# A hybrid decoder layer on one core: transposes of the second half in the products' PSUM banks, one head's loads on another queue, and two channel pairs of the up projection interleaved

## The chip, the cores and the metric

One NeuronCore of one Trainium2 chip. The metric is the device time of one execution in microseconds (us). Engines are named as in the profile: PE (TensorE, products and transposes), DVE (VectorE), ACT (ScalarE), POOL (GpSimd), SP (SyncE, which only issues DMAs here). PE's granted clock is given as a share of 2.4 GHz; its two levels are 1.00 (2.4 GHz) and 0.50 (1.2 GHz).

## The reference

One layer over 2048 tokens of width 1024, all in float32:

```python
h = rms(x, norm_mix_g);  z = h @ w_in + b_in            # columns for three groups of mixers
oa = forgetting_attention(rms(q), rms(k), v, cumsum(log_sigmoid(f)))   # 8 heads of 64
ob = mlstm_chunkwise(silu(conv4(b_qk)), b_v, b_i, b_f)                 # 4 heads of 64, chunks of 64
oc = hgrn2_chunkwise(silu(c_q), log_f, c_i)                            # 4 heads of 64, chunks of 16
y = concat(rms(oa), sigmoid(b_o) * rms(ob), silu(c_g) * rms(oc)) * out_g
x = x + y @ w_out
u = conv3(rms(x, norm_ffn_g) @ w_up) + conv_b;  gate, up = split(u)    # 2 x 2816 channels
out = x + (silu(gate) * up) @ w_down
```

## The kernel before

Every product of float32 operands is made of three products of split operands: `hi` (rounded, "fp32r") and `lo` (the rest), as hi·hi + lo·hi + hi·lo. ACT writes `hi`, and DVE or POOL subtracts to get `lo`.

**In-projection and mixers.** The tokens go in two halves of 1024, each of two blocks of 512. For a half, `z_norm` loads token tiles of 128 tokens (`z_load`, L225, a ring of two buffers tagged `x`), scales them (L163, DVE) and transposes them into `hhi`/`hlo` (`to_T`: eight transposes per tile in two groups of four, L174; ACT copies each group at L176, DVE subtracts at L177). The rstd of all eight tiles of the second half is made ahead by `z_stats`. `z_groups` then runs over 14 column groups of `w_in`; its products are at L215, 512 columns wide for the groups `c0 c1 b0 b1` and 256 narrow for the others. The product banks have the tag `w`, a ring of three in PSUM. The transposes of the norm and those of `qk_norm_T` (L427, which follow the q and k groups and wait for their own rstd chain) share the tag `t`, a ring of two; a `t` bank comes free when DVE has subtracted (L177 or L434).

`merge` runs the mixers' steps (mLSTM: L578 to L635; HGRN: L727 to L799) between the groups' steps: chains of small products on PE with work of DVE and ACT in between. The second half's first L727 needs the `c` columns of that half. Outside attention the order of instructions on each engine is the scheduler's, made when the kernel is built; attention's order is written out.

**Attention.** Eight heads in the order 4 5 6 7 0 1 2 3, over steps `t`. A step makes the scores of 128 keys by up to 512 queries (L936, L937; two PSUM banks tagged `s`), the exponential (L943) and a copy (L945) on ACT, the rest on POOL or DVE (L949), and, three steps later, the products with V (L962 to L964). `att_maxima` runs ahead (L886). `att_load` loads a head's QA, KA, QB, KB and V by ten DMAs from what the in-projection stored (`s_qh`, `s_kh`, `s_v`, ...), all on SP (L851); the next head's are issued at a written step, for the second head after the step (1, 2) of the first, the seventh. DMAs rotate over eight semaphores, so the ninth and tenth wait until the first and second have landed.

**Up projection.** The product by `w_up` is done by Strassen's scheme on 2 x 2 blocks: seven block products per pair of channel tiles (L1339), each 12 matmuls of 512 columns, named by the h-blocks `b11 b21 t1 t2 t3 t4 b22`. `up_blocks` loads four blocks of weights (L1302), makes four sums (L1313, DVE) and splits seven blocks (L1307 ACT, L1308 POOL). `h_unit` makes the h-blocks; `t3` and `b22` are split at its L1228 (DVE and POOL) while the first products run. `ffn_up` goes over pairs 0, 11, 1, 12, ...; a pair's two PSUM tiles (four in all) are emptied by the convolution (L1353 to L1355). For each pair of pairs POOL also makes sums of `w_down` (`w_blocks`, L1441).

## Time and profile before

| | us |
|---|---|
| median of 3 runs | 2878.68 (2875.48 to 2880.37) |
| profiled execution | 2879.12 |
| its span | 2877.0 (the other 2.1 lie around it) |
| PE busy | 2788.7, 97% |
| DVE, ACT, POOL busy | 1938.7 (67%), 1277.4 (44%), 1481.5 (51%) |
| mean granted clock of PE | 0.982 |

A row of the profile names a line of the code, an engine, what it writes and reads (out<-in) and times. "Idle before, releaser" is how long the engine stood before an instruction, and what ended that. A PE row's duration is longer than its share of time, since products overlap; the distance between starts is what one costs.

### The profile page before, as it was taken

What the parts mean: (1) busy time and instruction counts of PE and PEld (TensorE: products, weight loads), DVE (VectorE), ACT (ScalarE), POOL (GpSimd) and SP (SyncE); (2) the same over time, 40 slices, a digit from 0 to 9 for tenths busy, and PEclk for the clock granted to TensorE, in tenths of its full rate; (3) what the DMA queues carried; (4) which work ended last, traced back from release to release, by engine and by line L of the source; (5) the groups of instructions that cost most, each with busy time, mean ns of one, the idle gap of its engine ahead of it and who ended that gap; (6) DMA issues with size and microseconds to landing.
All of it is one profiled execution on the core that took longest, in us unless ns stands there. A gap on an engine that the chain in (4) does not pass through costs nothing. (4 is left out here: it accounts for less than half of the span.)

```text
span 2877.0 us, 42992 instructions
## 1 busy us (share of the span) xinstructions
PE 2788.7 (97%) x15053; PEld 2337.0 (81%) x15053; DVE 1938.7 (67%) x3523; ACT 1277.4 (44%) x2167; POOL 1481.5 (51%) x1451
## 2 busy tenths in 40 slices
PE   7999998999998999999999899999999999999999
PEld 7899996889997766776787688888788788888887
DVE  6336786264777787777446677776786677777655
ACT  4214322141322888888223444444454344434443
POOL 2346562344564678777001666665476445444443
PEclk9999997999998999999999999999999999999999
DMA  5424434333336534641456445545678333333766
GB/s 161 131 91 138 150 122 137 102 93 111 98 103 182 107 90 90 131 88 26 150 180 204 137 160 169 168 155 181 233 253 278 98 99 100 106 110 128 238 210 207
DMA packets 347160, 411.06 MB, mean 143 GB/s; under 512 B 47682, under 2 KB 234128, under 8 KB 344032
## 3 DMA queue, kind: packets, MB, share of 16 engines
q1 hardware_dynamic: 292560, 318.45, 37.3%
q10 hardware_dynamic: 51952, 81.45, 7.8%
q0 software_dynamic: 2432, 8.42, 0.8%
q8 instruction: 118, 1.93, 0.3%
q14 instruction: 98, 0.80, 0.1%
HBM read 280.24 MB, written 127.98 MB: 142 GB/s over the span
## 5 line engine op out<-in xcount | busy, mean ns | idle before, releaser
L1308 POOL TENSOR_TENSOR w<-w,w 128x512 fp32r<-128x512 f32 x302 | 403.2, 1349 | 404.6 <-ACT w L1307 349.4
L1496 PE MATMUL ps<-w,w 128*128 128x512 f32 x1848 | 423.3, 391 | 3.9 <-ACT w L1487 2.6
L1496 PEld LDWEIGHTS ps<-w,w 128*128 128x128 f32 x1848 | 348.2, 189 | 78.2 <-ACT w L1487 3.0
L215 PE MATMUL w<-whi,hhi 128*128 128x256 f32 (+1 forms) x1280 | 369.7, 289 | 2.7 <-DVE z L332 2.5
L215 PE MATMUL w<-wlo,hhi 128*128 128x256 f32 (+1 forms) x1280 | 370.2, 290 | 0.0
L215 PE MATMUL w<-whi,hlo 128*128 128x256 f32 (+1 forms) x1280 | 369.0, 288 | 0.0
L949 POOL TENSOR_TENSOR pl<-pf,ph 128x512 fp32r<-128x512 f32 (+2 forms) x240 | 288.4, 1218 | 110.1 <-ACT ph L945 73.7
L1489 POOL TENSOR_TENSOR w<-w,w 128x512 fp32r<-128x512 f32 x154 | 215.5, 1406 | 205.4 <-ACT w L1487 152.7
L1307 ACT ACTIVATE w<-w 128x512 fp32r<-128x512 f32 x302 | 180.7, 628 | 258.4 <-POOL w L1308 87.1
L1488 DVE TENSOR_TENSOR w<-w,w 128x512 fp32r<-128x512 f32 x154 | 177.0, 1159 | 110.1 <-ACT w L1486 103.9
L215 PEld LDWEIGHTS w<-whi,hhi 128*128 128x128 f32 x1280 | 245.0, 191 | 5.1 <-DVE z L332 3.0
L215 PEld LDWEIGHTS w<-whi,hlo 128*128 128x128 f32 x1280 | 244.8, 191 | 1.6 <-issue 0.2
L215 PEld LDWEIGHTS w<-wlo,hhi 128*128 128x128 f32 x1280 | 245.2, 192 | 0.7
L198 POOL TENSOR_TENSOR wlo<-wraw,whi 128x256 fp32r<-128x256 f32 (+1 forms) x224 | 171.7, 804 | 107.0 <-ACT whi L195 79.8
L1313 DVE TENSOR_TENSOR w<-w,w 128x512 f32<-128x512 f32 x176 | 149.6, 869 | 80.9 <-DMA w<-in_w_up_dram 74.3
L943 ACT ACTIVATE pf<-s 128x512 f32<-128x512 f32 (+1 forms) x320 | 172.2, 538 | 70.4 <-PE s L937 22.3
L945 ACT ACTIVATE ph<-pf 128x512 fp32r<-128x512 f32 (+1 forms) x320 | 185.1, 579 | 10.2
L901 DVE TENSOR_REDUCE mx<-m 128x1 f32<-128x512 f32 x192 | 130.6, 685 | 64.5 <-PE m L886 61.8
L1354 DVE SCALAR_TENSOR_TENSOR u<-ps,fcol,u 128x1023 f32<-128x1023 f32 x88 | 108.9, 1278 | 95.2 <-ACT u L1353 95.2
L1487 ACT ACTIVATE w<-w 128x512 fp32r<-128x512 f32 x154 | 96.6, 628 | 111.2 <-PE ps L1496 87.7
L1486 ACT ACTIVATE w<-w 128x512 fp32r<-128x512 f32 x154 | 95.9, 623 | 92.7 <-POOL w L1489 44.4
L886 PE MATMUL m<-KB,QB 70*128 70x512 f32 (+2 forms) x320 | 129.9, 415 | 3.4 <-DVE mx L890 3.4
(387 smaller groups left out, 7034.8 us busy)
## 6 DMA issues: line engine op xcount, KB each, us to landing
w<-in_w_up_dram SPq DMA_DIRECT2D x182, 256.0 KB
w<-s_g SPq DMA_DIRECT2D x154, 256.0 KB
w<-in_w_down_dram SPq DMA_DIRECT2D x110, 256.0 KB
wraw<-in_w_in_dram SPq DMA_DIRECT2D x48, 512.0 KB
s_g<-u ACTq DMA_DIRECT2D x88, 256.0 KB
w<-s_w SPq DMA_DIRECT2D x88, 256.0 KB
s_g<-w ACTq DMA_DIRECT2D x66, 256.0 KB
x<-in_x_dram SPq DMA_DIRECT2D x32, 512.0 KB
```

Source lines behind the costliest of these rows:

```text
L198: nc.gpsimd.tensor_tensor(lo[:, q + i, :], raw[:, i, :], h[:, i, :].bitcast(F32), op=ALU.subtract)
L215: nc.tensor.matmul(out, lsl(lhs[a], i), rsl(rhs[b], i), start=(i == 0 and j == 0), stop=(i == n - 1 and j == 2))
L901: nc.vector.tensor_reduce(mx[:, i, kb : kb + 1], m[:, 0:n], axis=AX.X, op=ALU.max)
L943: nc.scalar.activation(pf[:, c0:], s[:, c0:], AF.Exp)
L945: nc.scalar.activation(ph[:, c0:], pf[:, c0:], AF.Copy)
L949: eng.tensor_tensor(pl[:, c0:], pf[:, c0:], ph[:, c0:].bitcast(F32), op=ALU.subtract)
L1307: nc.scalar.activation(h, t, AF.Copy)
L1308: nc.gpsimd.tensor_tensor(lo, t, h.bitcast(F32), op=ALU.subtract)
L1313: nc.vector.tensor_tensor(t, x, y, op=op)
L1488: nc.vector.tensor_tensor(gl, gr, gh.bitcast(F32), op=ALU.subtract)
L1489: nc.gpsimd.tensor_tensor(wl, wr, wh.bitcast(F32), op=ALU.subtract)
L1496: nc.tensor.matmul(tiles[tile], g[x][:, tile * P : (tile + 1) * P], w[y], start=j == 0 and c == 0, stop=j == nj - 1 and c == 2,)
```

## The change

Three edits. (In the changed kernel lines stand a little lower: L727 is L728, L851 is L855, L943 is L947, L1339 is L1348, L1389 is L1397.) `norms_to_T` of the second half (both blocks) takes its transposes' banks from the tag `w` in place of `t`. `att_load` issues the second head's ten DMAs (n is 1) on ACT's queue in place of SP's. `ffn_up`'s loop body becomes a generator `channels`, which stops after the product `t1`; for the first pair of the first half the loop goes on to the second pair's first half before either's second half, and `up_blocks` splits the last three blocks only when `more` is called. A temporary (`u3`) is now written in place of `p1`.

```diff
 def to_T(...):
-        ps = k.t(psum, [P, 4, P], tag=ptag, bufs=2)
+        ps = k.t(psum, [P, 4, P], tag=ptag, bufs=2 if ptag == "t" else None)
 def z_norm(...):
-            norms_to_T(k, pz, psum, "t", [x], k.gmix, hi, lo, (t + i) * P, rstd[:, 4 * b + t + i : 4 * b + t + i + 1])
+            norms_to_T(k, pz, psum, "w", [x], k.gmix, hi, lo, (t + i) * P, rstd[:, 4 * b + t + i : 4 * b + t + i + 1])
 def att_load(...):
+    q = k.nc.scalar if n == 1 else k.nc.sync
     def ld(dst, src):
-        k.nc.sync.dma_start(dst.bitcast(F32), src)
+        q.dma_start(dst.bitcast(F32), src)
 def up_blocks(...):
-    for n, t in (("a11", a11), ("s2", s2), ("a12", a12), ("s1", s1), ("s3", s3), ("a22", a22), ("s4", s4)):
-        if n in names:
-            blocks[n] = parts(t)
-    return blocks
+    made = [("a11", a11), ("s2", s2), ("a12", a12), ("s1", s1), ("s3", s3), ("a22", a22), ("s4", s4)]
+    def make(some):
+        for n, t in some:
+            if n in names:
+                blocks[n] = parts(t)
+    make(made[:4])
+    return blocks, lambda: make(made[4:])
 def ffn_up(...):
+    def channels(p, early):
+        names = " ".join(n for n in ("a11", "s2", "a12", "s1", "s3", "a22", "s4") if n not in early)
+        w, more = up_blocks(k, fw, p, names)
...
         product(z, w["s1"], "t1")
+        yield
+        more()
         product(y, w["s3"], "t3", False)
-        u3 = tmp()
-        nc.vector.tensor_tensor(u3, y, p1, op=ALU.add)
-        nc.vector.tensor_tensor(y, z, u3, op=ALU.add)
+        nc.vector.tensor_tensor(p1, y, p1, op=ALU.add)
+        nc.vector.tensor_tensor(y, z, p1, op=ALU.add)
...
-        if p < NP // 2:
-            held = uu
+        held.append(uu)
+    held, begun = [], []
+    for i, p in enumerate(x for j in range(NP // 2) for x in (j, j + NP // 2)):
+        begun.append(channels(p, first if p == 0 else {}))
+        next(begun[-1])
+        if hf == 0 and i == 0:
+            continue
+        while begun:
+            next(begun.pop(0), None)
+        if len(held) < 2:
             continue
```

PE before, at the end of the first half's products: the last narrow products (L215), then the first tile's transposes (`x_4465`) among the mixers' products:

```order
L215 MATMUL w_5059<-whi_4636,hhi_545 128x256
L215 MATMUL w_5059<-wlo_4637,hhi_545 128x256
L215 MATMUL w_5059<-whi_4636,hlo_546 128x256
L796 MATMUL b_2961<-v_2087,c_kn_2959 128x128
L609 MATMUL b_2965<-bstate,b_qk_2637 128x130 x2
L788 MATMUL b_2982<-v_2087,att_2558 128x64
L174 MATMUL t_4806<-ident,x_4465 128x128 x4
L789 MATMUL b_2982<-cstate,q_94 128x64
L788 MATMUL b_2982<-v_2087,att_2558 128x64
L789 MATMUL b_2982<-cstate,q_94 128x64
L792 MATMUL b_2988<-ident,c_2552 128x128
L174 MATMUL t_4813<-ident,x_4465 128x128 x4
```

PE of the changed kernel, some 190 narrow products earlier in the first half, the same tile's transposes (now into `w` banks):

```order
L215 MATMUL w_4710<-wlo_4637,hhi_106 128x256
L215 MATMUL w_4710<-whi_4636,hlo_107 128x256
L174 MATMUL w_4806<-ident,x_4465 128x128 x4
L174 MATMUL w_4813<-ident,x_4465 128x128 x4
L758 MATMUL b_2786<-q_94,c_2552 128x128 x4
L561 MATMUL b_2803<-ident,rows_2798 128x12 x4
L569 MATMUL b_2812<-b_dec_405_2810,sel_773 128x4 x2
L215 MATMUL w_4821<-whi_4469,hhi_545 128x256
```

and at the end of the first half's products, the fourth tile's transposes and the first second-half products (`128x512`):

```order
L215 MATMUL w_5059<-whi_4636,hlo_546 128x256
L174 MATMUL w_5153<-ident,x_5041 128x128 x4
L174 MATMUL w_5160<-ident,x_5041 128x128 x3
L790 MATMUL b_2982<-cstate,q_94 128x64
L789 MATMUL b_2982<-v_2087,att_2558 128x64
L790 MATMUL b_2982<-cstate,q_94 128x64
L793 MATMUL b_2988<-ident,c_2552 128x128
L174 MATMUL w_5160<-ident,x_5041 128x128
L797 MATMUL b_2992<-v_2087,c_kn_2990 128x128
L622 MATMUL b_2996<-v_2792,e_2887 128x65 x4
L789 MATMUL b_3042<-v_2087,att_2558 128x64
L215 MATMUL w_5183<-hhi_4803,whi_5167 128x512
L215 MATMUL w_5183<-hlo_4804,whi_5167 128x512
```

The four tiles of the second half's first block are now transposed by the end of the first half's products (before: after it, among the mixers' chain), and the wide products follow at once. From the start of the first second-half transposes to the second half's first L727, PE's program holds 96 wide products before; after the change it holds the last 192 narrow products of the first half, then 192 wide and 96 narrow ones of the second.

ACT before, around the seventh exponential (`s_10116`) of attention, with the semaphores that each instruction waits for:

```order
L943 ACTIVATE pf_10099<-s_10096 128x512 [waits PE_49,Pool_49]
L945 ACTIVATE ph_10101<-pf_10099 128x512 [waits Activation_49]
L943 ACTIVATE pf_10119<-s_10116 128x512 [waits PE_49,Pool_49]
L945 ACTIVATE ph_10121<-pf_10119 128x512 [waits Activation_49]
L943 ACTIVATE pf_10153<-s_10150 128x512 [waits DVE_49,PE_49]
L945 ACTIVATE ph_10155<-pf_10153 128x512 [waits Activation_49]
L970 ACTIVATE oT_10168<-pv_10073 65x512
```

and of the changed kernel, at the same place:

```order
L947 ACTIVATE pf_10119<-s_10116 128x512 [waits PE_49,Pool_49]
L949 ACTIVATE ph_10121<-pf_10119 128x512 [waits Activation_49]
L855 DMA QB_10137<-s_qh 64x2048 [waits DMAHW3_49]
L855 DMA KB_10138<-s_kh 64x2048 [waits DMAHW4_49]
L855 DMA QB_10137<-s_one 6x2048 [waits DMAHW5_49]
L855 DMA KB_10138<-s_one 4x2048 [waits DMAHW6_49]
L855 DMA KB_10138<-s_fc 2x2048 [waits DMAHW7_49]
L855 DMA QA_10135<-s_qh 64x2048 [waits DMAHW0_49]
L855 DMA QA_10135<-s_ql 64x2048 [waits DMAHW1_49]
L855 DMA KA_10136<-s_kl 64x2048 [waits DMAHW2_49]
L855 DMA KA_10136<-s_kh 64x2048 [waits DMAHW3_49]
L855 DMA V_10139<-s_v 128x16x130 [waits DMAHW4_49]
```

The ten loads stand between the seventh copy and the eighth exponential; the first and the ninth wait for the same semaphore (DMAHW3), and so do the second and the tenth (DMAHW4).

PE before, in the up projection: the end of the first pair's twelve `t3` products, which follow its `t1` products directly (`ps_17898`, `ps_17899` are the first pair's banks; `ps_18049`, `ps_18050` the second's):

```order
L1339 MATMUL ps_17899<-t3h,w_17890 128x512
L1339 MATMUL ps_17899<-t3l,w_17890 128x512
L1339 MATMUL ps_17899<-t3h,w_17891 128x512
L1339 MATMUL ps_18049<-b11h,w_18021 128x512
L1339 MATMUL ps_18049<-b11l,w_18021 128x512
L1339 MATMUL ps_18050<-t2h,w_18025 128x512
L1339 MATMUL ps_18050<-t2l,w_18025 128x512
L1339 MATMUL ps_17898<-b22h,w_17894 128x512
L1339 MATMUL ps_17898<-b22l,w_17894 128x512
```

and of the changed kernel (`ps_17890`, `ps_17891` the first pair's banks; `ps_17988`, `ps_17989` the second's), from the first pair's last `t1` product on:

```order
L1348 MATMUL ps_17890<-t1h,w_17887 128x512
L1348 MATMUL ps_17988<-b11h,w_17972 128x512
L1348 MATMUL ps_17988<-b11l,w_17972 128x512
L1348 MATMUL ps_17989<-t2h,w_17976 128x512
L1348 MATMUL ps_17989<-t2l,w_17976 128x512
L1348 MATMUL ps_17891<-t3h,w_18042 128x512
L1348 MATMUL ps_17891<-t3l,w_18042 128x512
L1348 MATMUL ps_17988<-b11h,w_17973 128x512
L1348 MATMUL ps_17988<-b11h,w_17972 128x512
```

Only two of the first pair's twelve `t3` products stand ahead of the second pair's first half now (b11, t2, b21, t1, 48 products); the other ten and `b22` stand behind it. On POOL, the second pair's a11 and s2 parts now follow the four `b22l` and one sum of `w_down`; on DVE, the third pair's four sums stand ahead of the first pair's L1397 (before: L1389).

## Rows read from the trace of the kernel before

**Rows 1.** The page: the busy line (busy time, share of the span and instructions of each engine; the part for PE and the others), and the shares of the chain that ended last by line.

```profile
PE 2788.7 (97%) x15053; PEld 2337.0 (81%) x15053; DVE 1938.7 (67%) x3523; ACT 1277.4 (44%) x2167; POOL 1481.5 (51%) x1451
...
PE ps L1339 26%; PE ps L1496 14%; PE w L215 2%; POOL w L1308 1%; DMA w<-s_h 0%; DMA w<-in_w_up_dram 0%; DVE w L1313 0%; DVE u L1355 0%; DVE u L1354 0%; DMA w<-s_g 0%; ACT u L1353 0%; DMA w<-in_w_down_dram 0%; DMA s_g<-u 0%; DVE t3l L1228 0%; PE tn L1192 0%
```

**Rows 2.** Busy time of each engine by stretch: from and to, length, then busy us of PE, its weight loads, DVE, ACT and POOL with their instructions, the granted clock of PE, the DMA engines' share and GB/s.

```profile
300.00:400.00 100.00, 98.84 (x823) 95.94 (x821) 79.63 (x198) 29.21 (x51) 53.35 (x73) 1.00 0.44 141
400.00:430.00 30.00, 28.77 (x228) 26.78 (x228) 26.29 (x51) 10.11 (x17) 24.39 (x29) 1.00 0.28 89
430.00:480.00 50.00, 37.21 (x178) 30.28 (x177) 39.83 (x107) 16.01 (x28) 14.45 (x26) 0.63 0.41 131
480.00:500.00 20.00, 20.00 (x93) 16.43 (x92) 9.92 (x24) 4.75 (x8) 3.74 (x7) 0.91 0.50 171
500.00:520.00 20.00, 16.86 (x80) 14.02 (x79) 11.21 (x17) 5.11 (x9) 4.85 (x6) 0.91 0.20 66
910.00:940.00 30.00, 22.38 (x89) 16.00 (x88) 21.68 (x60) 8.18 (x16) 16.88 (x27) 0.66 1.00 262
1590.00:1620.00 30.00, 21.36 (x77) 14.86 (x76) 22.51 (x19) 11.41 (x21) 25.17 (x17) 0.84 0.56 171
```

**Rows 3.** What PE waited for in 430 to 520 (total us, times, longest).

```profile
PE t L174 <- DVE l L434: 3.4, 1, 3.4
PE b L727 <- DVE q L723: 3.1, 1, 3.1
```

**Rows 4.** Timeline of PE around the half boundary: start, us, line, what it writes and reads, how many alike in a run, and the wait ahead of it. From 501.70 to 506.01 twenty products of 512 columns stand in a row (first and last shown), with 19 steps between their starts.

```profile
429.50 0.28 PE L215 MATMUL w<-whi,hhi 128*128 128x256 f32 x1
...
429.62 0.28 PE L215 MATMUL w<-wlo,hhi 128*128 128x256 f32 x1
...
430.70 0.61 PE L174 MATMUL t<-ident,x 128*128 128x128 f32 x4
...
481.33 1.22 PE L215 MATMUL w<-hhi,whi 128*128 128x512 f32 x2
...
501.70 0.39 PE L215 MATMUL w<-hlo,whi 128*128 128x512 f32 x1
...
506.01 0.40 PE L215 MATMUL w<-hhi,wlo 128*128 128x512 f32 x1
...
510.42 1.95 PE L727 MATMUL b<-q,c 128*128 128x256 f32 x5 [3.14 <-DVE q L723]
```

**Rows 5.** Costliest groups of DVE in 395 to 520: busy us and mean ns of one.

```profile
L177 DVE TENSOR_TENSOR hlo<-t,hhi 128x512 fp32r<-128x512 f32 x16 | 10.7, 686 | 3.8 <-ACT hhi L176 3.5
L163 DVE SCALAR_TENSOR_TENSOR x<-x,n8r,gmix 128x1024 f32<-128x1024 f32 x7 | 9.9, 1411 | 7.8 <-DMA x<-in_x_dram 7.8
```

**Rows 6.** What PE waited for in 910 to 935.

```profile
PE s L936 <- ACT pf L943: 4.0, 1, 4.0
```

**Rows 7.** ACT at the start of attention (the first exponential with the wait ahead of it, and the seventh copy), and the DMA instructions on the tensor `s_v` in 900 to 940 (how long the issue takes in ns, first and last start; the last line is from issue to landing of both kinds).

```profile
930.41 0.60 ACT L943 ACTIVATE pf<-s 128x512 f32<-128x512 f32 x1 [13.18 <-DMA s_v<-x]
...
940.65 0.63 ACT L945 ACTIVATE ph<-pf 128x512 fp32r<-128x512 f32 x1
...
L348 POOL DMA_DIRECT2D s_v<-x x4: 552/564/596, 909.9 to 923.3; - x4
...
DMA to landing us min/median/max: 3.7/6.2/7.8
```

**Rows 8.** SP's issues of `att_load`: the first of the second head, and the first and the last of the ten of the sixth head.

```profile
919.90 0.91 SPq L851 DMA_DIRECT2D QB<-s_qh  x1
...
1149.57 0.45 SPq L851 DMA_DIRECT2D QB<-s_qh  x1
...
1156.98 0.39 SPq L851 DMA_DIRECT2D V<-s_v  x1
```

**Rows 9.** PE in attention (second products of two steps that follow each other), and the stretch after PE's wait of 507 to 510, as in rows 2.

```profile
938.22 0.40 PE L937 MATMUL s<-QA,KA 128*128 128x512 f32 x1
...
939.52 0.40 PE L937 MATMUL s<-QA,KA 128*128 128x512 f32 x1
...
510.50:515.00 4.50, 4.50 (x18) 3.81 (x19) 2.73 (x6) 1.10 (x2) 2.64 (x4) 0.62 0.27 90
```

**Rows 10.** ACT in the up projection: an activation that waited, and the DMA issue that came out behind it (ACTq is ACT's sequencer).

```profile
1621.08 1.21 ACT L1353 ACTIVATE u<-ps,fcol 128x1024 f32<-128x1024 f32 x1 [6.92 <-DVE ps L1395]
1621.15 0.34 ACTq L1442 DMA_DIRECT2D s_w<-w  x1
```

**Rows 11.** POOL at the start of the up projection.

```profile
1594.83 6.27 POOL L1308 TENSOR_TENSOR w<-w,w 128x512 fp32r<-128x512 f32 x4 [57.46 <-ACT w L1307]
...
1601.06 6.78 POOL L1228 TENSOR_TENSOR b22l<-w,b22h 128x512 fp32r<-128x512 f32 x4
...
1607.80 1.73 POOL L1441 TENSOR_TENSOR w<-w,w 128x512 f32<-128x512 f32 x1
...
1614.53 2.50 POOL L1441 TENSOR_TENSOR w<-w,w 128x512 f32<-128x512 f32 x2
```

**Rows 12.** What PE waited for in 1585 to 1625.

```profile
PE ps L1339 <- DVE t3l L1228: 4.0, 4, 2.4
PE ps L1339 <- DVE ps L1390: 2.8, 1, 2.8
```

**Rows 13.** PE's first `t3` product of the first pair.

```profile
1601.16 0.39 PE L1339 MATMUL ps<-t3h,w 128*128 128x512 f32 x1
```

More of the change, by code (lines that the diff above doesn't have):

```diff
@@ L1362, in conv, with tmp @@
         return u
-    held = None
-    for p in (x for j in range(NP // 2) for x in (j, j + NP // 2)):
-        early = first if p == 0 else {}
-        w = up_blocks(k, fw, p, " ".join(n for n in ("a11", "s2", "a12", "s1", "s3", "a22", "s4") if n not in early))
+    def tmp():
+        return k.t(fw, [P, BLK], tag="tmp", bufs=4)
+    def channels(p, early):
+        names = " ".join(n for n in ("a11", "s2", "a12", "s1", "s3", "a22", "s4") if n not in early)
+        w, more = up_blocks(k, fw, p, names)
         w.update(early)
@@ L1370, in ffn_up @@
         x, z, wd, y = g[:, :BLK], g[:, BLK:], u[:, :BLK], u[:, BLK:]
-        def tmp():
-            return k.t(fw, [P, BLK], tag="tmp", bufs=4)
         product(x, w["a11"], "b11")
-        p1 = tmp()
+        p1, u2 = tmp(), tmp()
         nc.scalar.activation(p1, x, AF.Copy)
@@ L1381, in ffn_up @@
         product(y, w["s2"], "t2")
-        u2 = tmp()
         nc.vector.tensor_tensor(u2, y, p1, op=ALU.add)
@@ L1386, in ffn_up @@
         product(z, w["s1"], "t1")
+        yield
+        more()
         product(y, w["s3"], "t3", False)
-        u3 = tmp()
-        nc.vector.tensor_tensor(u3, y, p1, op=ALU.add)
-        nc.vector.tensor_tensor(y, z, u3, op=ALU.add)
+        nc.vector.tensor_tensor(p1, y, p1, op=ALU.add)
+        nc.vector.tensor_tensor(y, z, p1, op=ALU.add)
         if not early:
             product(wd, w["a22"], "t4")
-        nc.vector.tensor_tensor(wd, u3, wd, op=ALU.subtract)
+        nc.vector.tensor_tensor(wd, p1, wd, op=ALU.subtract)
         product(z, w["s4"], "b22", False)
@@ L1406, in ffn_up @@
             w_blocks(k, j)
-        g_blocks(k, hf, j, held, uu)
+        g_blocks(k, hf, j, held.pop(0), held.pop(0))
 def ps_tile(k, shape):
```

## The prediction

> **What bounds the kernel now.** I read the busy line and the chain first [rows 1]: TensorE (PE) is busy 97% of the span, and the chain that ended last runs through its product lines. So an edit pays only where PE stands idle or runs below full clock, and the next view is PE's busy time and granted clock by stretch [rows 2]. An ordinary stretch, 300 to 400, has PE at 98.84 of 100 us at clock 1.00. Three stretches do not, and each holds one part of the change. I count what each loses as its idle time plus busy time times (1 - clock):
>
> - Half boundary, 400 to 520: idle 1.2 + 12.8 + 0 + 3.1 = 17.1; clock 37.21 x 0.37 + 20.0 x 0.09 + 16.86 x 0.09 = 17.1. Together 34 us.
> - Start of attention, 910 to 940: 7.6 + 22.38 x 0.34 = 15 us.
> - Start of the up projection, 1590 to 1620: 8.6 + 21.36 x 0.16 = 12 us.
>
> The waits [rows 3] name little at the boundary (3.4 behind a `t` bank, 3.1 behind L723), because many short stalls and a half-speed clock make up the rest. The timeline [rows 4] shows the cause: the first norm transpose stands at 430.70, the first second-half product at 481.33. For those 51 us PE has only the mixers' dependent little products and the transposes.
>
> **Part A, transposes in the products' banks.** No work is added or removed. What moves is the order of PE: the first tile's transposes now stand ahead of the last 192 narrow products of the first half (some 396 us in the old trace), and second-half products follow the last first-half product at once. The price can be counted up to one common point, the first L727 of the second half (510.42 before). By the listing, 96 wide products (512 columns) stand between the boundary and L727 before; after the change 192 wide and 96 narrow ones (256) do. A wide one takes (506.01 - 501.70) / 19 = 0.227 us, a narrow one 429.62 - 429.50 = 0.12 us [rows 4]. So 96 x 0.227 + 96 x 0.12 = 33.3 us of work is done earlier, into time that PE lost. From 396 to L727 the new order holds 34 (to 430) + (51 + 29 - 33, the work of the old stretch without its losses) + 33 = about 114 us of PE work, so L727 falls near 510 again and the 33 us come out as gain, less what PE still waits. The mixers' chain is not asked to run faster than before; it only gets cover.
>
> What could spoil it is VectorE (DVE): 26.3 us of work in 400 to 430, 39.8 + 9.9 + 11.2 in 430 to 520 [rows 2], some 87 with the edges. In 114 us that is 76%, as in the ordinary stretch (79.63 of 100, where PE loses 1.2%). But it is not even: each norm tile costs DVE 1.41 + 2 x 0.69 = 2.8 us [rows 5], and L163 of three tiles and L177 of four (3 x 1.41 + 8 x 0.69 = 9.7 us) move into 396 to 430, where DVE had 3.7 us free. They push mixer work back by some 6 us; products cover it. A transposed half tile also holds one of the three product banks until ScalarE and then DVE (0.69 [rows 5]) have emptied it, about 2 us with the transposes, while a wide product of 24 steps fills 5.4 us; the other two banks suffice unless DVE is late by more. I take 1.4 us for the ordinary rate and 3 us for one such wait with a short fall of the clock: **A = -29**. Bounds: -34 (all that is lost), and -15 if DVE, at 8 to 9 tenths, leaves half of the stalls.
>
> **Part B, the second head's ten loads on ScalarE (ACT).** No bytes change. Before, SP issues them from 919.90 on [rows 8], while the last stores of the previous phase are under way; the first exponential stood 13.2 us behind the store of V [rows 7], and PE 4.0 us behind that exponential [rows 6]. Now they stand after the seventh exponential and copy in ACT's program. At that point (the seventh copy, 940.65 before) the stores are down: the last was issued at 923.3 and took 7.8 us at most [rows 7]. The stores took 6.2 us in the middle and 3.7 at best [rows 7]; without this traffic I put the last one 3 us sooner: -3, bounds 0 and -4 (with an undisturbed clock -8).
> The other side: ten issues with two landings in between (KA's second load waits on QB's, V on KB's) took 1149.57 to 1156.98 plus 0.39 = 7.8 us on SP for a later head [rows 8]. In ACT's queue all later exponentials wait behind them. PE goes on for two steps (two score banks), 939.52 - 938.22 = 1.3 us each [rows 9]. So PE stands 7.8 - 2.6 + 0.6 = about 5.5 us. After the 3.1 us stall at 507 the clock was 0.62 for 4.5 us [rows 9], 1.7 us of work; I add that. ACT cannot regain it, since PE is the limit again afterwards. **B = -3 + 5.5 + 1.7 = +4**. Bounds -8 (the stores decide, the issue hides) and +12 (both stalls with a longer half-speed clock).
> ACT's queue is in order for this: L1353 started at 1621.08 and the DMA issue behind it at 1621.15 [rows 10], though POOL had finished its data by 1617 (1614.53 + 2.50 [rows 11]). The Trainium skill, Perfetto Trace Analysis, section "DVE / Act Engine Instruction (TENSOR_ADD, Activation, etc)", has an instruction wait in a queue of its own while the sequencer goes on to the next. By that the ten loads would leave as early as before and hold up little: B near 0, the sum 4 us lower. The trace speaks against it here.
> The Trainium skill, DMA: Bandwidth & Descriptors, section "Issuing engines are not separate DMA queues", says that loads from any engine share the same 16 DMA engines. By that the new queue itself wins nothing, only the later moment does; without my -3 the sum would be 3 us higher.
>
> **Part C, the first two channel pairs together.** The products are the same. Before, PE waited 4.0 us for `t3l` and 2.8 for L1390 [rows 12], since POOL was solid from 1594.83: four block parts (6.27), four `b22l` (6.78), then w_down sums (1.73) [rows 11]. Now the second pair's first half is to fill that, but its blocks come from the same POOL: two parts 3.1, four `b22l` 6.8, one sum 1.7, then a11's part 1.6: together 13.2 us from 1594.8, so 1608. PE has done `t1` by 1601.2 (the old first `t3` product [rows 13]) and has six products more, to 1602.6, so it stands 5.5 us once, then runs through (each next part, at 1.6, and the sums between keep near the 12 x 0.23 = 2.8 us that its product takes). 5.5 + 0.5 of waits and 2 for the clock (1.7 at 507) are 8 instead of 12: **C = -4**. Bounds -8 and +4, the latter if the third pair's sums, which now stand ahead of the first pair's L1397 on DVE, come late with their loads.
>
> **Sum.** -29 + 4 - 4 = -29 on 2879.1 (2877.0 span and 2.1 around it): 2850. The profiled execution is within 0.5 of the median, so this stands for it too. About 0.2% (5.8 us) is what a measurement can tell from no change.
>
> **Rivals.**
> 1. *B and C pay too.* ACT's issues hide behind PE's two steps and the store decides: A -33, B -4, C -6, so 2836. For: the first stall is due to a store alone. Against: 7.8 us of issue. 0.13.
> 2. *DVE becomes the bound at the boundary.* For: it was busy 26.3 of the 30 us ahead of the boundary already, and gets 9.7 us more there. Against: its share over the whole stretch. A gives -15, the sum is -15: 2864. 0.19.
> 3. *The bank was not what held the order in time:* the norm's loads and DVE's L163 come no sooner, PE waits at the transposes at 396 to 430 instead. A -4, B +4, C -4: 2875, no change. Against: DVE's L163 has its rstd long before, and the wait named at a transpose is for a bank [rows 3]. 0.06.
> 4. *Slower: transposes hold product banks.* Sixteen half tiles; if each keeps PE from its next product by t, A is -33 + 16 t. With t = 2.5 (DVE having four instructions ahead of the eviction each time) that is +7, the sum 2886. It decides from t = 2.4 (2885). Against: PE waited for a `t` bank once, 3.4 us, with a ring of two [rows 3]. 0.05.
> 5. *ACT's issues run ahead of its waiting exponentials.* The first one waits 13.2 us [rows 7], into which 7.8 us of issues fit; then the loads leave about as early as before and nothing is held up. B 0, 2846. Against: [rows 10]. 0.08. The section of Perfetto Trace Analysis named above would have it so.
>
> My forecast has the rest, 0.49, and its own range is 2844 to 2857. The range 2835 to 2868 takes in rivals 1, 2 and 5. Faster than 2873: 0.88 (forecast, 1, 2, 5 less 0.01); same 0.07; slower 0.05.
>
> **What would show it.** Right: second-half products from about 430, PE over 96% in 400 to 520 at clock near 1, L727 still near 510; first exponential some 3 us earlier relative to the phase's end, then a gap of 7 to 8 us between the seventh copy and the eighth exponential, PE idle 5 in it; one PE stall near five us in the up projection in place of several. Wrong: PE waiting for L177 or L176 on `w` banks, DVE at ten tenths from 400 on, no gap on ACT, or a late L1397.

## The result, and the profile after

| | before | after |
|---|---|---|
| median, us | 2878.86 (2875.48 to 2884.49, 6 runs) | 2890.01 (2884.74 to 2894.23, 6 runs) |
| profiled execution, its span | 2879.12, 2877.0 | 2888.28, 2885.4 |

The ratio is 1.0030 (95%: 1.0018 to 1.0042): the change made the kernel slower by 5 to 12 us, where 2850 was predicted. Medians, here and below, leave out two executions in a far slower state (one at 3124 us of the kernel with its loads late on SP, one at 4583 us of the kernel before).

The page's busy line of the changed kernel (as in [rows 1]):

```profile
PE 2788.1 (97%) x15053; PEld 2335.5 (81%) x15053; DVE 1945.9 (67%) x3523; ACT 1276.6 (44%) x2167; POOL 1482.0 (51%) x1451
```

The work is the same. The stretches, with the columns of [rows 2] (length, then busy us of PE, its weight loads, DVE, ACT, POOL, the granted clock, the DMA share, GB/s):

```profile
390.00:430.00 40.00, 33.81 (x256) 31.20 (x254) 37.50 (x69) 12.77 (x20) 23.12 (x28) 0.96 0.33 105
400.00:430.00 30.00, 25.97 (x187) 23.78 (x187) 27.57 (x48) 9.82 (x15) 18.52 (x23) 0.94 0.32 101
430.00:480.00 50.00, 43.03 (x227) 36.77 (x227) 31.87 (x81) 14.42 (x28) 13.22 (x23) 0.80 0.41 127
...
500.00:520.00 20.00, 20.00 (x97) 15.88 (x96) 7.71 (x17) 6.87 (x9) 6.68 (x9) 1.00 0.23 81
910.00:940.00 30.00, 20.56 (x69) 13.49 (x68) 17.56 (x42) 7.31 (x14) 11.71 (x16) 0.67 0.67 167
940.00:945.00 5.00, 4.10 (x16) 2.99 (x16) 2.21 (x5) 3.73 (x7) 1.78 (x2) 0.50 1.00 208
1590.00:1620.00 30.00, 23.51 (x86) 16.95 (x85) 18.36 (x17) 12.11 (x22) 22.58 (x16) 0.83 0.62 193
1640.00:1650.00 10.00, 8.80 (x26) 6.54 (x27) 10.00 (x12) 7.50 (x12) 5.29 (x3) 0.69 0.08 28
```

Against [rows 2], PE is fuller from 430 to 480 (43.03 for 37.21, clock 0.80 for 0.63), but emptier ahead of the boundary (25.97 for 28.77 in 400 to 430). In attention there is a stretch at clock 0.50 (940 to 945), and the up projection has a second dent at 1640 to 1650.

The balance can be read from landmarks, the starts of instructions that every kernel has. Single traces differ even where the code is the same: kernels with the code of before up to attention begin it at 913.7 to 917.5; the distance in the second row is 35.3 to 41.1 in the nine kernels below that leave part B's code as it was, and that in the third row 430.1 to 432.0 in the nine that leave part C's.

| us | before | after |
|---|---|---|
| first product of attention's maxima (L886; L890 after) | 913.7 | 905.7 |
| from there to the 16th score step | 38.0 | 45.6 |
| from the first L1339 (L1348) to the first L1496 (down projection) | 430.3 | 439.1 |

So by these two traces A gained 8, B cost 7.6 and C 8.8, for terms of -29, +4 and -4. The first two are uncertain by some 4 us, the third by 1 to 2.

### The profile page after: what moved, and what is told of

Same layout as the page of the kernel before. It is cut to its first block, busy times and chain, and to the rows that moved or that the text cites. A ratio compares the mean times of both kernels' runs of the same rounds, so it can differ in the third digit from the quotient of the medians.

```text
span 2885.4 us, 42990 instructions
## 1 busy us (share of the span) xinstructions
PE 2788.1 (97%) x15053; PEld 2335.5 (81%) x15053; DVE 1945.9 (67%) x3523; ACT 1276.6 (44%) x2167; POOL 1482.0 (51%) x1451
## 5 line engine op out<-in xcount | busy, mean ns | idle before, releaser
L215 PE MATMUL w<-whi,hhi 128*128 128x256 f32 (+1 forms) x1280 | 372.6, 291 | 3.2 <-DVE hlo L177 1.7
L215 PE MATMUL w<-wlo,hhi 128*128 128x256 f32 (+1 forms) x1280 | 372.2, 291 | 0.0
L215 PE MATMUL w<-whi,hlo 128*128 128x256 f32 (+1 forms) x1280 | 371.0, 290 | 0.0
L215 PEld LDWEIGHTS w<-whi,hhi 128*128 128x128 f32 x1280 | 247.4, 193 | 5.6 <-DVE hlo L177 2.1
L215 PEld LDWEIGHTS w<-whi,hlo 128*128 128x128 f32 x1280 | 246.9, 193 | 1.7 <-issue 0.3
L215 PEld LDWEIGHTS w<-wlo,hhi 128*128 128x128 f32 x1280 | 247.2, 193 | 1.1 <-issue 0.2
L1317 DVE TENSOR_TENSOR w<-w,w 128x512 f32<-128x512 f32 x176 | 155.8, 903 | 84.0 <-DMA w<-in_w_up_dram 72.6
L947 ACT ACTIVATE pf<-s 128x512 f32<-128x512 f32 (+1 forms) x320 | 172.1, 538 | 77.5 <-PE s L941 23.7
L1363 DVE SCALAR_TENSOR_TENSOR u<-ps,fcol,u 128x1023 f32<-128x1023 f32 x88 | 109.0, 1279 | 90.4 <-ACT u L1362 90.4
L940 PE MATMUL s<-QB,KB 70*128 70x512 f32 (+1 forms) x320 | 125.2, 391 | 10.1 <-ACT pf L947 10.1
```

Source lines behind the costliest of these rows:

```text
L215: nc.tensor.matmul(out, lsl(lhs[a], i), rsl(rhs[b], i), start=(i == 0 and j == 0), stop=(i == n - 1 and j == 2))
L947: nc.scalar.activation(pf[:, c0:], s[:, c0:], AF.Exp)
L1317: nc.vector.tensor_tensor(t, x, y, op=op)
```

## The experiments

Each kernel was timed against the kernel before on the same chip; the medians of before there were 2882.5 to 2883.4.

### Each part by itself

A alone, B alone and C alone: the diff's hunks for `to_T` and `z_norm`, for `att_load`, and for `up_blocks` and `ffn_up`.

A alone:

> Part A alone. Theory (the three parts add up, read from the two traces against the same amount of PE work done): the changed kernel is 8 us ahead of the kernel before when attention starts, after a loss of 11 us in 390 to 430 and a gain of 20 in 430 to 520; so alone it ends 6 to 10 us faster, 2870, with the same loss ahead of the boundary. Rival (the start of attention waits for stores that come no sooner, so a gain made before them is given back there): 2876 to 2881. The prediction's own step had -29, 2850.

B alone:

> Part B alone. Theory: the last store of V lands no sooner without the second head's loads beside it (7 us from issue to landing, as before), so nothing is won, and the ten issues hold ACT for 7.3 to 8 us, PE for 5 and its clock for some more: 6 to 9 us slower, 2887. The prediction's step: the store 3 us sooner, 4 us slower in all, 2883.

C alone:

> Part C alone. Theory: the single stall near 1603 to 1610 gains 2 us, then the third pair's first product waits for the first pair's banks (all four are taken by two pairs in flight, and their convolution comes late on DVE): 3 to 4 us there, its half-speed clock, and 2 more at the fifth pair; 9 us slower in all, 2888. The prediction's step: 4 us faster, 2875.

| | median, us | ratio (95%) |
|---|---|---|
| A | 2873.22 | 0.9967 (0.9954 to 0.9979), 9.3 us faster |
| B | 2889.91 | 1.0022 (1.0011 to 1.0033), 7.4 slower |
| C | 2891.02 | 1.0030 (1.0018 to 1.0043), 8.5 slower |

Together +6.6, which the whole change's +5 to +12 holds: the parts add up as far as this can tell. Each interval reaches some 3 us to either side, so that one part hides a few us of another is not excluded.

### Part A: what eats two thirds of the gain

The second half's first L728 of the changed kernel stands at 536.29, and the same line of A alone at 534.74, where 510.42 stood before [rows 4]. The prediction counted 33.3 us of work done earlier if that landmark stays; A alone leaves 33.3 - 24.3 = 9.0, and 9.3 were measured. That the two agree to 0.3 is partly luck, since kernels with the order of before have the landmark at 510.4 to 513.8. That the work moved is seen from the other side too: from the landmark to the start of attention A alone takes 369.7 us for 403.3, 33.6 less. So the order of the work is as predicted, and the missing 20 us are PE's waits and slow clock ahead of the landmark. The rows of PE in the changed kernel (the third tile's transposes, the first second-half product, and the landmark):

```profile
426.34 0.60 PE L174 MATMUL w<-ident,x 128*128 128x128 f32 x4
430.98 1.02 PE L174 MATMUL w<-ident,x 128*128 128x128 f32 x4 [4.04 <-DVE hlo L177]
...
451.71 0.80 PE L215 MATMUL w<-hhi,whi 128*128 128x512 f32 x1 [0.26 <-DVE hlo L177]
...
536.29 1.89 PE L728 MATMUL b<-q,c 128*128 128x256 f32 x8
```

Second-half products begin at 451.71, where 481.33 stood before [rows 4] and about 430 was predicted. On the way PE stands 4.04 us for the one `w` bank that L177 has to free. ACT had its copy of that bank (L176) done at 427.58, so 2.66 of the 4.04 us are DVE's lateness: L177 starts at 430.24. DVE in that time, and its next L333:

```profile
426.15 0.70 DVE L132 TENSOR_TENSOR hu<-rstd 128x16 f32<-128x16 f32 x1
426.89 0.65 DVE L133 TENSOR_TENSOR hu<-hu,hh 128x16 f32<-128x16 f32 x1
427.57 0.65 DVE L134 SCALAR_TENSOR_TENSOR rstd<-hu,rstd 128x16 f32<-128x16 f32 x1
428.25 0.65 DVE L132 TENSOR_TENSOR hu<-rstd 128x16 f32<-128x16 f32 x1
428.93 1.18 DVE L133 TENSOR_TENSOR hu<-hu,hh 128x16 f32<-128x16 f32 x1
430.15 0.18 DVE L134 SCALAR_TENSOR_TENSOR rstd<-hu,rstd 128x16 f32<-128x16 f32 x1
430.24 0.68 DVE L177 TENSOR_TENSOR hlo<-w,hhi 128x512 fp32r<-128x512 f32 x1
...
439.45 1.29 DVE L333 TENSOR_TENSOR z<-w,bias 128x512 f32<-128x512 f32 x2 [2.54 <-PE t L428]
```

and POOL beside it:

```profile
423.82 3.68 POOL L198 TENSOR_TENSOR wlo<-wraw,whi 128x256 fp32r<-128x256 f32 x5
427.47 1.40 POOL L818 TENSOR_TENSOR p<-p,gbc 128x256 f32<-128x256 f32 x2
428.83 1.26 POOL L542 TENSOR_TENSOR b_qk<-c,c 128x512 f32<-128x512 f32 x1
430.41 2.32 POOL L424 TENSOR_TENSOR z<-z,rstd 128x256 f32<-128x256 f32 x4 [0.32 <-DVE rstd L134]
```

In DVE's program the L333 of two groups of narrow products, which PE had done by 426.5, stand behind that tile's L177. They run at 439.45, so two of the three banks hold finished products until then, and one is left for both of the tile's transposes. The wait that their row names, 2.54 us, is for PE's L428, which reads the tile that L333 is to overwrite; L428 needs POOL's L424, and that was released only at 430.41, by the end of the chain of small steps in the rows above. Ahead of L177 stand six steps of a norm's rstd chain, on 16 columns. While POOL works they start 0.68 to 0.74 us apart, the length of one POOL instruction (3.68 / 5 = 0.74), and the one beside POOL's 1.26 takes 1.18; the last, with POOL idle from 430.09, takes 0.18. The Trainium skill, SBUF — State Buffer, section "SBUF: two separate sides", says that DVE and POOL share one pair of ports under an exclusive lock held for a whole instruction, and that a DVE instruction with two SBUF inputs needs it against a POOL instruction that reads SBUF; these rows agree, and L177, which reads one input from PSUM, keeps its 0.68. That these slow small steps are what makes L177 late is read from the rows; no run takes the slowness away by itself.

What PE waited for `w` banks until L177 had freed them, in 380 to 545:

```profile
PE w L174 <- DVE hlo L177: 4.2, 2, 4.0
...
PE w L215 <- DVE hlo L177: 1.9, 3, 1.2
```

These are 6.1 of the 14.0 us of waits that this view names; the next are 2.9 us for ACT's L795 and 2.2 for ACT's L286, and between 430 and 480 the clock of 0.80 takes 8.6 more.

Two theories were left: DVE is late ahead of the boundary, or three product banks are too few for products and transposes. The first is tested by taking L163 (1.3 to 1.4 us per tile) off DVE, the second by a fourth `w` bank, taken from `t`, which then has one.

A with four `w` banks (the other tiles of the tag `t` get one bank in the same way):

```diff
-        ps = k.t(psum, [P, 4, P], tag=ptag, bufs=2 if ptag == "t" else None)
+        ps = k.t(psum, [P, 4, P], tag=ptag, bufs=1 if ptag == "t" else None)
-            psw = pool(zs, "psw", 3, space=PSUM)
+            psw = pool(zs, "psw", 4, space=PSUM)
```

> Part A alone, with four product banks (tag w) and one bank for the transposes of q and k (tag t) in the whole in-projection. If the loss of 11 us in 390 to 430 is for want of product banks (transposed tiles hold them), a fourth takes the waits for L177 and for the copies away: the loss falls to 4 to 6 and the gain over before grows from 9 to 13 to 15 us. If it is DVE that is late with everything, the mixers' chain too, one more bank changes little: 8 to 10 us ahead of before, as A alone; and the single t bank can cost a few us in the q and k groups.

A with the second half's scaling on ACT (the norm's gain is left out there):

```diff
-        nc.vector.scalar_tensor_tensor(x, x, rstd[:, i : i + 1], gb, op0=ALU.mult, op1=ALU.mult)
+        if ptag == "w":
+            nc.scalar.activation(x, x, AF.Copy, scale=rstd[:, i : i + 1])
+        else:
+            nc.vector.scalar_tensor_tensor(x, x, rstd[:, i : i + 1], gb, op0=ALU.mult, op1=ALU.mult)
```

> Part A alone, with the second half's norm scaling (L163) taken from DVE: ACT scales by rstd instead, and the norm's gain is left out, so that 8 x 1.4 = 11 us of DVE's work are gone, three tiles' 4 us of them ahead of the boundary. If DVE is the bound there: the loss in 390 to 430 falls from 11 to 5 or 6 us, and the gain over before grows from 9 to 14 or more. If DVE's load is not it (banks, the order itself): within 2 us of A alone.

Four banks: 2883.66, ratio 1.0000 (0.9989 to 1.0011). Scaling on ACT: 2854.20, 0.9900 (0.9884 to 0.9916), 28.6 us faster. The stretches of the latter:

```profile
390.00:430.00 40.00, 36.20 (x285) 34.11 (x284) 34.44 (x73) 16.77 (x24) 21.60 (x26) 0.96 0.35 108
430.00:480.00 50.00, 48.98 (x307) 41.35 (x307) 31.71 (x90) 22.93 (x39) 19.23 (x36) 1.00 0.60 190
```

DVE is at 34.44 of 40 us ahead of the boundary in place of 36.83 in A alone (37.50 in the changed kernel), and PE at 48.98 of 50 at full clock behind it.

The four banks do not decide the question by their total, since the single `t` bank also serves the start of the kernel: PE is busy 74.7 of the first 100 us there, for 83.5 before, with 10.6 us of waits for L177 at the transposes (3.9 before). So that run is read between two instructions with the same work between them: the 2051st product at L215, ahead of the boundary, and the second half's first L727. In A alone these stand at 385.23 and 534.74, with four banks at 403.27 and 548.25: 149.5 us and 145.0. So the fourth bank is worth some 4.5 us at the boundary, in a measure in which the seven traces with the order of before spread over 3.3.

Two more kernels separate the bank from the relief, and make the relief legal. In the first, L163 of the second half goes to ACT (gain left out) while the transposes stay in `t`:

```diff
+    act = rstd is not None
-        nc.vector.scalar_tensor_tensor(x, x, rstd[:, i : i + 1], gb, op0=ALU.mult, op1=ALU.mult)
+        if act:
+            nc.scalar.activation(x, x, AF.Copy, scale=rstd[:, i : i + 1])
+        else:
+            nc.vector.scalar_tensor_tensor(x, x, rstd[:, i : i + 1], gb, op0=ALU.mult, op1=ALU.mult)
```

> The kernel before with the scaling on ACT (the norm's gain left out) and the transposes still in the banks of the tag t. If both are needed (banks to bring the transposes ahead, DVE relieved to let them through): the first wide product still stands near 480 and the run gains 2 to 6 us only. If the relief of DVE alone does it: 20 us or more faster, and the banks do not matter.

In the second, which computes all, A and the scaling on ACT are joined by the gain, multiplied into the second half's weights by ACT as they are loaded (the same edit at the other call of `load_split`, and the loading of `k.gn`, are left out here):

```diff
-def load_split(k, wp, src, n=4):
+def load_split(k, wp, src, n=4, gain=False):
+        if gain:
+            for i in range(n):
+                nc.scalar.activation(raw[:, i, :], raw[:, i, :], AF.Copy, scale=k.gn[:, q + i : q + i + 1])
-        w = load_split(k, wp, w_in[:, off : off + width])
+        w = load_split(k, wp, w_in[:, off : off + width], gain=hf == 1)
```

> The whole computation again: part A, the second half's norm scaled by rstd on ACT, and the norm's gain multiplied into the rows of the second half's weights by ACT (four small activations per load, 14 x 2 x 4 = 112 of them in 430 to 900, where ACT is busy three tenths). If DVE's scaling was what held part A back, the 28 us of the run without the gain stay but for a few: 22 to 28 us faster than before, about 2856. If the added activations delay the weights' copies: 10 to 18 us faster.

The first: 2879.83, 0.9984 (0.9972 to 0.9996), 3.6 us faster. What PE waits for most in its 430 to 520:

```profile
PE b L731 <- DVE q L727: 4.3, 1, 4.3
```

That is the wait that ended at 510.42 before [rows 4]; here it ends at 506.88, 3.5 us sooner, and that is all the relief alone gives. The second: 2861.98, **0.9926 (0.9913 to 0.9940), 21.4 us faster than the kernel before**, the best full kernel of the study. Its stretches:

```profile
390.00:430.00 40.00, 38.49 (x318) 36.06 (x316) 35.78 (x78) 19.31 (x31) 25.82 (x34) 1.00 0.37 119
430.00:480.00 50.00, 47.81 (x293) 40.43 (x291) 32.70 (x92) 29.53 (x56) 14.64 (x28) 0.99 0.63 193
```

All five together, with the prediction's measure of loss (idle time plus busy time times (1 - clock)), over 390 to 520, and with the time from the 2051st L215 to the first L727, which holds 33.3 us more work where the transposes are in `w` (the gain is 33.3 less what the time grew). Before has this row ahead of the boundary:

```profile
390.00:430.00 40.00, 38.77 (x315) 36.66 (x315) 35.54 (x70) 12.05 (x20) 28.99 (x33) 1.00 0.27 87
```

| | lost in 390:520 | saved of it | L215 to L727 | gain by that | measured gain (medians) |
|---|---|---|---|---|---|
| before | 34 | | 124.2 | | |
| A | 22.5 | 12 | 149.5 | 8.0 | 9.3 |
| A, four `w` banks | (boundary 13 us later) | | 145.0 | 12.5 | 0 (13.5 behind by 100 us) |
| A, scaling on ACT, no gain | 6.4 | 28 | 132.2 | 25.3 | 28.6 |
| A, scaling on ACT, gain in the weights | 5.4 | 29 | 131.6 | 25.9 | 21.4 |

The prediction's -29 left 4.4 us of loss. It is nearly reached once DVE has room, with three banks. The full kernel gives some 5 us back later in the in-projection: from the landmark to the start of attention it takes 375.1 us, where A alone takes 369.7 and the kernel without the gain 370.5. Its 112 scalings of weights take ACT 0.495 us each, and PE waits there in many small pieces; which of them is the scalings' doing was not taken apart.

### Part B: the block, the moment or the queue

In the changed kernel ACT does what was predicted at the ten issues (ACTq is its sequencer):

```profile
921.91 0.60 ACT L947 ACTIVATE pf<-s 128x512 f32<-128x512 f32 x1 [12.51 <-DMA s_v<-x]
...
932.29 0.63 ACT L949 ACTIVATE ph<-pf 128x512 fp32r<-128x512 f32 x1
932.29 0.50 ACTq L855 DMA_DIRECT2D QB<-s_qh  x1
...
939.76 0.39 ACTq L855 DMA_DIRECT2D V<-s_v  x1
940.25 0.60 ACT L947 ACTIVATE pf<-s 128x512 f32<-128x512 f32 x1 [7.33 <-DMA QB<-s_one]
```

The first issue starts with the seventh copy, not ahead of it, and the next exponential starts 0.1 us after the last issue has ended. PE's waits in 900 to 960, the first of them ahead of the ten issues, the second behind:

```profile
PE s L940 <- ACT pf L947: 10.1, 2, 5.1
```

The second one ends at 940.90, and the 5 us behind it run at clock 0.50 (window above).

The store: the last issues of `s_v` on POOL, as in [rows 7]:

```profile
913.57 1.09 POOL L349 DMA_DIRECT2D s_v<-x  x2
```

From there to the first exponential it is 921.91 - 913.57 = 8.3 us after. Before it was 930.41 - 922.75 = 7.7 (930.41 is in [rows 7]; 922.75 starts the same last pair). The start of attention is as far from the store as it was. In the nine kernels whose loads leave early the same distance is 7.7 to 10.8, in the middle 8.3; in the four whose loads leave late it is 7.1 to 8.3, in the middle 7.3.

To tell apart the late moment, the new queue and the block, the loads were left on SP but made late (five one-column clears on DVE of the tiles to be loaded, at the written step, which the loads then follow), and put on ACT one per step:

```diff
+    if n == 1:
+        for t in (QA, KA, QB, KB):
+            k.nc.vector.memset(t[0:64, 0:1].bitcast(F32), 0.0)
+        k.nc.vector.memset(V[:, 0, 0:1].bitcast(F32), 0.0)
```

> The kernel before, with the second head's ten loads still on SP, but behind five small writes of DVE into their tiles at the same written step as in the change, so that they leave SP only then (the writes are overwritten by the loads). If it is the place on ACT's queue that costs: no ACT gap, PE idle at the start of attention as before, time within 3 us of before. If it is the late moment (the loads' traffic beside the first steps): 4 to 9 us slower as with part B. If the stores gain by the quiet queues, as the prediction had it: 3 us faster, and the first exponential 3 us sooner after the last store's issue.

```diff
+    q = k.nc.scalar if n == 1 else k.nc.sync
     for x in first:
         ld(*x)
+        if n == 1:
+            yield
 ...
-                            for _ in att_load(k, h + 1, sts[h + 1]):
-                                pass
+                            if h == 0:
+                                second = att_load(k, 1, sts[1])
+                        if second is not None:
+                            next(second, None)
```

> Part B alone, with the ten loads on ACT's queue spread over ten steps, one behind each step's copy, from the same step on. If it is the block of ten issues that costs: no PE stall over 1 us after the seventh step, ten issues of 0.5 us between exponentials that have some room, within 2 us of the kernel before (0 to +2). If any issue on ACT's queue at this place costs (ACT is busy 87% of the time in attention): 4 to 6 us slower.

Late on SP: 2881.05, 0.9993 (0.9984 to 1.0002). One per step on ACT: 2881.40, 0.9994 (0.9985 to 1.0004). PE's waits for exponentials at the start of attention, for B alone, late on SP, and spread on ACT:

```profile
PE s L938 <- ACT pf L945: 8.5, 2, 5.2
```

```profile
PE s L941 <- ACT pf L948: 3.2, 1, 3.2
```

```profile
PE s L949 <- ACT pf L956: 3.5, 1, 3.5
```

Only the block has the second wait. On SP in the late version, the same ten loads go out after ACT's seventh copy as well:

```profile
943.91 0.45 SPq L856 DMA_DIRECT2D QB<-s_qh  x1
...
951.33 0.39 SPq L856 DMA_DIRECT2D V<-s_v  x1
```

From the first start to the last end it is 7.8 us, as it was on ACT (7.9), now in a queue where nothing else waits. And spread on ACT, each issue starts together with a copy and the next exponential follows within the usual step:

```profile
942.09 0.50 ACTq L853 DMA_DIRECT2D QB<-s_qh  x1
942.70 0.60 ACT L956 ACTIVATE pf<-s 128x512 f32<-128x512 f32 x1
...
955.15 0.38 ACTq L853 DMA_DIRECT2D V<-s_v  x1
```

So the late moment wins little if anything (both medians are 1.4 us lower, and both intervals take in no change), ACT's queue costs nothing measurable by itself, and the block of ten costs the 7 us: attention's first maxima to its 16th score step takes 38.0 before, 45.6 with B, 37.3 late on SP and 38.1 spread (35.3 to 41.1 where part B's code is as before).

### Part C: the stall moves to the banks

PE's long waits in the changed kernel's up projection:

```profile
1603.58 0.50 PE L1348 MATMUL ps<-b11h,w 128*128 128x512 f32 x1 [2.58 <-ACT w L1311]
...
1606.04 0.79 PE L1348 MATMUL ps<-t2h,w 128*128 128x512 f32 x1 [1.73 <-ACT w L1311]
...
1628.94 0.50 PE L1348 MATMUL ps<-b22h,w 128*128 128x512 f32 x1 [1.17 <-DVE ps L1398]
...
1640.85 0.79 PE L1348 MATMUL ps<-b11h,w 128*128 128x512 f32 x1 [3.45 <-ACT halo L1366]
```

The first two are the predicted stall for the second pair's blocks: 2.58 and 1.73, with 0.83 and 0.55 at 1608 and 1610 it is 5.7 us. The third is what is left of the 2.8 us for L1390 before [rows 12]; the fourth is new. Ahead of them on PE, the first of the first pair's other ten `t3` products, and then DVE and ACT:

```profile
1622.62 0.62 PE L1348 MATMUL ps<-t3h,w 128*128 128x512 f32 x2
```

```profile
1620.81 6.75 DVE L1317 TENSOR_TENSOR w<-w,w 128x512 f32<-128x512 f32 x4 [2.67 <-DMA w<-in_w_up_dram]
1627.48 0.68 DVE L1397 TENSOR_TENSOR tmp<-ps,tmp 128x512 f32<-128x512 f32 x1
...
1639.31 1.27 DVE L1364 SCALAR_TENSOR_TENSOR u<-ps,fcol,u 128x1022 f32<-128x1022 f32 x1
```

```profile
1640.62 0.17 ACT L1366 ACTIVATE halo<-ps 128x2 f32<-128x2 f32 x1 [5.58 <-DVE u L1364]
```

The third pair's four sums (1.69 each beside POOL; one of the same kind with POOL idle took 0.69, at 1637.51) stand ahead of the first pair's L1397, after a wait of 2.67 for their loads. L1397 comes at 1627.48, for 1613.36 before. The sums are the smaller part of that: the last ten of the `t3` products that L1397 needs start only at 1622.62, behind the second pair's 48, and at 0.227 us each they end near 1625, so the sums hold L1397 by some 2.5 us. The convolution of the first pair gives its first PSUM tile free with the halo copy, at 1640.79, after an L1364 ahead of which DVE waited 1.65 us more for the loads of the sum at 1637.51. The third pair writes into the first pair's tiles. Before, the first pair's convolution had the whole second pair's products to end in; now half of those stand ahead of the first pair's own end, two pairs fill all four tiles, and PE has nothing else in its program.

Two kernels test this. In one, the convolution of the first pair is made shorter: C with DVE's two taps (L1363 and L1364) left out for that pair's two channel tiles.

```diff
-        nc.vector.scalar_tensor_tensor(u[:, 1:], ps[:, :-1], cw(1), u[:, 1:], op0=ALU.mult, op1=ALU.add)
-        nc.vector.scalar_tensor_tensor(u[:, 2:], ps[:, :-2], cw(0), u[:, 2:], op0=ALU.mult, op1=ALU.add)
+        if hf == 1 or ct not in (0, NP):
+            nc.vector.scalar_tensor_tensor(u[:, 1:], ps[:, :-1], cw(1), u[:, 1:], op0=ALU.mult, op1=ALU.add)
+            nc.vector.scalar_tensor_tensor(u[:, 2:], ps[:, :-2], cw(0), u[:, 2:], op0=ALU.mult, op1=ALU.add)
```

> Part C alone, with DVE's two convolution taps left out for the first pair's two channel tiles (a part of the computation that is missing there), so that the first pair's banks come free after ACT. If the third pair waits for those banks: PE's waits of 2.9 and 2.6 us near 1641 to 1649 and the slow clock behind them go, and of the 9 us lost 5 to 6 come back: 3 to 4 us slower than before. If the third pair's late weights are the cause: the same loss under another name, 8 us slower.

In the other, C keeps its generator and the temporary in place but not the interleaving:

```diff
         next(begun[-1])
-        if hf == 0 and i == 0:
-            continue
         while begun:
```

> Part C without its interleaving: generator, split in two steps and the temporary written in place stay, but the second pair begins after the first is through. If the two pairs in flight cost the 9 us: within 2 us of the kernel before, PE's waits at 1600 to 1620 as before, none for banks at 1640. If the split or the temporary written in place costs: 5 us or more slower.

Without the taps: 2887.64, 1.0017 (1.0008 to 1.0027), 4.9 us slower. Without the interleaving: 2884.29, 1.0002 (0.9992 to 1.0011). The waits for the halo in C alone (1590 to 1665):

```profile
PE ps L1344 <- ACT halo L1362: 5.5, 2, 2.9
```

and those of the kernel without the taps (the first stands in their place, the second is in C alone too, with 1.5):

```profile
PE ps L1344 <- ACT tmp L1382: 2.5, 1, 2.5
PE ps L1344 <- DVE ps L1395: 1.4, 1, 1.4
```

The first L1339 to the first L1496 takes 430.3 before, 440.4 with C, 435.3 without the taps, 430.4 without the interleaving. So the interleaving costs all of it, and the late release of the first pair's banks up to half (3.6 of 8.5 by the medians, 5 of 10 by the landmarks; leaving out the taps also takes four instructions of 1.28 us off DVE). The rest stands behind waits for the first pair's `b22` and for a copy of the temporary, and was not taken apart further.

## Why the prediction was wrong

**The bound, the places and the order** were right: the three parts act where they were put, and within the noise they add up. Each failed on one step.

**Part A: the mechanism was right, the term was mis-sized, by the step "They push mixer work back by some 6 us; products cover it".** 33.3 us of work moved as counted. But the first half's products ended at 443.84 for 429.62 [rows 4], second-half products began at 451.71 for about 430, and "L727 falls near 510 again" did not hold: it fell at 536. The text saw that DVE had 3.7 us free ahead of the boundary and would get 9.7 more, and then went by the mean over 114 us, 76%. PE's program there has the new transposes between products, so a late L177 holds not just a bank but PE itself (4.04 us), with the products that should have been the cover standing behind. "The other two banks suffice unless DVE is late by more" failed with it: the other two were full, since DVE's L333 was late too. The duration of DVE's small instructions was not priced at all: five that take 0.17 to 0.18 us alone took 0.65 to 1.18 beside POOL. That is rival 2, which had the right place and cause; it put A at -15, and -9.3 was measured. Rival 4's price per half tile did not come: L174 and L215 waited 4.2 + 1.9 = 6.1 us for L177, 0.4 us for each of sixteen, far from 2.4. Rival 3 fell too: the order in time did change. The scaling on ACT then showed the mechanism at its full size.

**Part B: the issue's side held, the store's did not.** The block was put at 7.8 us, PE's stall at 5.5 (its own terms, 7.8 - 2.6 + 0.6, give 5.8) and the clock's loss at 1.7; measured were 7.33 of waiting ACT, 5.10 of PE, and 4.10 busy us at clock 0.50, 2.1 lost: 7.2 in all, and 7.4 by the medians of B alone. That time, with its interval of 3 to 10 us, would not exclude the +4; the rows decide. The step that failed is "without this traffic I put the last one 3 us sooner": the last store was as far from the first exponential as before (8.3 us, and 8.3 in A alone, whose loads went out early on SP; in the order of before 7.2 in B alone and 7.1 late on SP, for 7.7 to 10.8 in the four kernels whose loads left early: some 1 us in the middle, and none in the changed kernel). The median of the stores' landings was taken for what the last one would do. Rival 1 rested on the same step. Rival 5 fell: the first issue came out with the seventh copy, so ACT's sequencer does not run ahead of its waiting instructions here, as [rows 10] had it.

**Part C: the first stall held, "then runs through" did not.** One stall of some 5.5 us was predicted and stands at 1603 to 1610. The bound on the other side named a late L1397, but put it down to the third pair's sums and their loads and at +4; it was +8.5, and most of L1397's lateness is the ten `t3` products behind the second pair's 48 (the sums hold it by some 2.5 us). What the step left out is that two pairs in flight own all four PSUM tiles. A late L1397 then delays not only `b22` (1.17, less than the 2.8 of before) but the whole convolution, and with it the third pair's first product (3.45 in the changed kernel, 2.9 in C alone), and the clock falls again (0.69 in 1640 to 1650).

**The sum by what was measured**: -9.3 + 7.4 + 8.5 = +6.6.

## What to carry to other kernels

When work moves to a busier place, price it in the window it moves into, not over the stretch: count the engine's free time in the 30 us ahead of the spot, and what each of its instructions costs beside its neighbour engine there. A reordering that fills PE needs the engine that frees the banks to be on time; here the reordering alone gave 9 us, the relief alone 4, and both 21 to 29. Before a block of issues goes into a compute engine's queue, spread it one per step, and before two units of work are put in flight, count the banks that the third one needs and what stands ahead of their release.

## What the runs showed of the hardware

- DVE instructions on 16 columns with both inputs in SBUF took 0.17 to 0.18 us alone and 0.65 to 1.18 beside POOL, at the pace of POOL's own instructions; one with a single input (L124, at 422.50) took 0.70 too. Sums of 512 columns took 0.69 and 1.69. So a chain of tiny instructions lost most: six steps took 4.18 us, five of them beside POOL.
- Ten DMA issues take 7.8 to 7.9 us in a queue, on SP and on ACT alike; on ACT 2.7 of it were waits ahead of the ninth and the tenth. One issue beside each of ACT's copies cost nothing that could be measured (0.9994, 0.9985 to 1.0004).
- Taking other loads out of the way of the last store brought the instruction that waits for it forward by some 1 us of 8.3 in the middle (7.1 to 8.3 in four kernels, 7.7 to 10.8 in nine), not by 3.
